# Weight halves by casting and accumulating DMAs, a pair's sums on VectorE, and plain quarters in tiles that stand empty: a two-layer hybrid decoder trunk on one core

## The chip, the cores and the metric

The kernel runs on one NeuronCore of one Trainium2 chip. The metric is device time in microseconds (us) of one execution. Engines are named as the profile names them: PE is TensorE's matmul side and PEld its weight load, DVE is VectorE, ACT is ScalarE, POOL is GpSimd, SP is SyncE. SPq is SP's queue, which issues DMAs here.

## The reference

Two layers over 512 tokens and 1024 channels, all in float32:

```python
h = rmsnorm(x, norm_g[layer])
u = h @ w_in[layer]                 # one projection: q, k, v, z of three mixers and gates ga, gb, gc
ya = forgetting_attention(...)  * silu(za)      # 4 heads, dense causal
yb = dilated_mixture(...)       * silu(zb)      # 6 heads, rotary
yc = banded_attention(...)      * silu(zc)      # 6 query and 2 key heads, rotary, window 128
merged = (sigmoid(ga) * (ya @ w_br_a[layer]) + sigmoid(gb) * (yb @ w_br_b[layer])
          + sigmoid(gc) * (yc @ w_br_c[layer]))
x = x + merged @ w_out[layer]
...
return rmsnorm(x, final_norm_g)
```

## The kernel before, in words

Every product of a weight with activations is made of three float32r matmuls (`mm3`, L127 to L129): a float32 value is split into a rounded half `h` and the rest `lo = x - h`, and `wh*xh + wh*xl + wl*xh` is summed in PSUM. So each weight has to reach SBUF as two tiles, `wh` and `wl`. A weight comes in **chunks** of at most 128x520 (a unit of the input projection is two chunks of 128x512, a branch projection `p` is one of 128x256 or 128x384). The order in which PE uses the chunks is `seq`. One call of `dma()` (L1066) loads chunks ahead through SP into five `raw` tiles, and `split_to()` (L1109) makes the halves up to six chunks ahead of PE: ACT casts `wh <- raw` (L1116) and DVE subtracts `wl <- raw - wh` (L1118; POOL does so for the last output projection). Both rings hold six tiles (`RING`).

In each layer the order of work is: the `v` chunks (eight, with tokens on the PSUM partitions), the `f` chunks (four), then seventeen steps `h` of the attention heads with projections in between, then the merge items. `m_item` ("solo") makes a gate unit `g` (24 matmuls of 512 columns) and a branch product `p` (6 or 9), each in its own PSUM bank of the three called `mm`. Its evacuation is L629 (DVE, `g` times `rbc`), L630 (ACT), L636 or L639 (DVE, with `p`), and for branch 1 a merge into `mg` on POOL (L641).

The last twelve gates of a layer are made two at a time by `pair_steps`, by a Winograd form of Strassen's scheme: seven products of 4 x 3 matmuls of 256 columns instead of eight. A pair uses nine chunks in this order: forms w0, w1, w2, w3, then branch p, then w4, w5, branch p, w6. Forms 0, 1 and 4 are plain quarters of the gate weights (B11, B21, B22); forms 2, 3, 5 and 6 are sums of quarters, made by `source()`: L1101 on DVE, L1103, L1104 and L1106 on POOL. The banks `att` hold the products `a`, `b` and `c`; e1 (L728), e5 (L735) and e2 (L738) are ACT's copies out of them, and product 3 writes the bank that e1 reads. The merge is L707 (POOL, but DVE in the last pair), then ACT's cast L718 and DVE's L719 split the merged gate for the output projection. There are two pairs of branch 1 and four of branch 2 in a layer.

The pairs need sums of activations too. `sums(l, k)`, k = 0 to 3, loads two slices of x (L591), scales them on ACT (L592), forms four sums on POOL and DVE in turn (L600 POOL, L601 DVE, L602 POOL, L603 DVE) and splits them (L607 ACT, L608 DVE). Three of the four stand right before the last two solo items.

Each engine runs its instructions in the order in which they are issued. Python runs ahead, and the tile framework adds the waits and decides from priorities what is issued when (`urgent` raises it).

Of the kernel before, what the change touches and what calls it, by code (L numbers as in the profile page):

```python
# [7 lines left out]
F32 = mybir.dt.float32  # L8
# [19 lines left out]
RING = 6  # L28
RAW = 5
# [35 lines left out]
def tile_trunk(ctx: ExitStack, tc: tile.TileContext, xT, wpk, gT, gfT, bfg, snk,  # L65
# [24 lines left out]
    def tmp():  # L90
        return T([P, S], F32, "tmp", 7)

# [436 lines left out]
    def pv_item(l, h, pair):  # L529
# [30 lines left out]
        def rest():  # L560
            ys = st["ys"]
            nc.vector.tensor_tensor(ys, ys, st["sz", pair], op=ALU.mult)
            if pair < 6:
                yh, yo = T([P, S], F32R, "y", 10), T([P, S], F32R, "y", 10)
# [20 lines left out]
    def sums_x(l, k):  # L585

        src = xT if l == 0 else x1d
        d = []
        for kk in (k, k + 4):
            t = tmp()  # L590
            nc.sync.dma_start(t, src[:, kk, :])  # L591
            nc.scalar.activation(t, t, AF.Copy, scale=g_sb[:, l, kk:kk + 1])  # L592
            d.append(t)
        return d

    def sums(l, k):
        def run():
            a, b = sums_x(l, k)
# [14 lines left out]
    def m_item(l, br, i):  # L613
# [18 lines left out]
        def p2():  # L632
# [7 lines left out]
            if br == 1:  # L640
                nc.gpsimd.tensor_tensor(m, m, gr, op=ALU.add)  # L641
                return
            nc.vector.tensor_tensor(m, m, gr, op=ALU.add)
            pair = []
            for w in range(2):
                n = 2 * i + w
                pair.append(T([P, S], F32R, "qk", 12) if n < 12 else T([P, S], F32R, "y", 10))
            nc.scalar.copy(pair[0], m)
            nc.vector.tensor_tensor(pair[1], m, rd(pair[0]), op=ALU.subtract)
            st["MH", i], st["ML", i] = pair  # L650
        return unit(l, COL["g" + "abc"[br]] + P * i) + [("p", l, br, i)], pe, p1, p2, None

    def pair_steps(l, br, i, last=False):
# [48 lines left out]
        def merge(u, c):  # L702
            def run():
# [3 lines left out]
                (nc.vector if last else nc.gpsimd).tensor_tensor(m, m, gr, op=ALU.add)  # L707
                if br < 2:
                    return
                if ("MH", i + u, l) not in d:  # L710
                    d["MH", i + u, l] = True
                    pair = []
                    for w in range(2):
                        q = 2 * (i + u) + w
                        pair.append(T([P, S], F32R, "qk", 12) if q < 12 else T([P, S], F32R, "y", 10))
# [172 lines left out]
    def layer(l):  # L888
# [79 lines left out]
        for h in range(17):  # L968
            A = items_of(f"a{h}") if h else []
            B = items_of(f"b{h}")  # L970
            if h:
# [4 lines left out]
                if h == 16:  # L976
                    do(sums(l, 3))
# [23 lines left out]
            if h < 15:  # L1001
                do(sscale)
            if h == 16:
                do(vrest)
# [15 lines left out]
        for k in (2, 0, 1):  # L1020
            do(sums(l, k))
        solo(M(1, 2))
        solo(M(1, 3))
# [19 lines left out]

    seq = [c for it in items for c in it[0] or ()]
    loads, at = [], {}
    for i, key in enumerate(seq):
        if key[0] == "w":
            _, l, br, u, form = key
            if form == 0:
                c = [COL["g" + "abc"[br]] + P * (u + w) for w in range(2)]  # L1050
                for name, blk, last in (("B11", ("u", l, c[0], 0), 3), ("B12", ("u", l, c[1], 0), 6),
                                        ("B22", ("u", l, c[1], 1), 6), ("B21", ("u", l, c[0], 1), 8)):
                    loads.append(dict(name=(key[:4], name), blk=blk, tag="raw", last=i + last, since=0))
        else:
            pair = i > 0 and key[0] == "p" and any(k[:3] == ("w", key[1], key[2]) and k[3] in (key[3], key[3] - 1)
                                                   for k in seq)
            since = next(n for n, k in enumerate(seq) if k == ("w", key[1], key[2], key[3] // 2 * 2, 0)) + 1 if pair else 0
            loads.append(dict(name=key, blk=key, tag="sz" if pair else "raw", last=i, since=since))
    order, raw, hl = {"raw": [], "sz": []}, {}, {}
    for n, d in enumerate(loads):  # L1060
        d["turn"] = len(order[d["tag"]])
        order[d["tag"]].append(n)
    ptr = dict(dma=0, split=0)

    def dma(slack=0, most=1 << 30):

        while ptr["dma"] < min(len(loads), most):
            d = loads[ptr["dma"]]
            tag = d["tag"]
            bufs = RAW if tag == "raw" else 2  # L1070
            before = d["turn"] - bufs + (slack if tag == "raw" else 0)
            if ptr["split"] < d["since"]:
                return
            if before >= 0 and loads[order[tag][before]]["last"] >= ptr["split"]:
                return
            o, w = off[d["blk"]]
            t = raw[d["name"]] = T([P, CH], F32, "raw", RAW) if tag == "raw" else T([P, S], F32, "sz", 2)
            nc.sync.dma_start(t[:, :w], bass.AP(tensor=wpk.tensor, offset=wpk.offset + o,
                                                ap=[[w, P], [1, w]]))
            ptr["dma"] += 1  # L1080

    def places(key):

        n = 2 * key[2] + key[3] if key[:2] == ("o", L - 1) else 0
# [167 lines left out]
```

## Time and profile before

| | |
|---|---|
| median of 3 runs (lowest, highest) | 903.9 us (903.22, 904.86) |
| the profiled execution, its own time | 905.74 us |
| its span, first to last instruction | 904.0 us |
| mean granted TensorE clock | 0.988 of full speed |
| DMA traffic | 93.53 MB, mean 103 GB/s |

The profile is of one execution, 1.8 us slower than the median. Shares of busy time are averages over stages; PE is called busy while any of its pipelined matmuls is under way.

### The profile page before, as it was taken

What the parts mean: (1) busy time and instruction counts of PE and PEld (TensorE: products, weight loads), DVE (VectorE), ACT (ScalarE), POOL (GpSimd) and SP (SyncE); (2) the same over time, 40 slices, a digit from 0 to 9 for tenths busy, and PEclk for the clock granted to TensorE, in tenths of its full rate; (3) what the DMA queues carried; (4) which work ended last, traced back from release to release, by engine and by line L of the source; (5) the groups of instructions that cost most, each with busy time, mean ns of one, the idle gap of its engine ahead of it and who ended that gap; (6) DMA issues with size and microseconds to landing.
All of it is one profiled execution on the core that took longest, in us unless ns stands there. A gap on an engine that the chain in (4) does not pass through costs nothing.

```text
span 904.0 us, 14292 instructions
## 1 busy us (share of the span) xinstructions
PE 871.9 (96%) x4866; PEld 754.7 (83%) x4866; DVE 706.2 (78%) x1402; ACT 508.0 (56%) x1072; POOL 212.4 (24%) x162
## 2 busy tenths in 40 slices
PE   9999999999999799899999999999999997998996
PEld 6988888888888599888888888888888876998895
DVE  7668899988787798994446879999878769988643
ACT  7467566655565554554336856576556645544552
POOL 5000231200001545431110012212100035554531
PEclk9999999999999899999999999999999998999998
DMA  6622323323224233345442232233222342322433
GB/s 215 193 84 72 115 70 89 106 78 98 67 63 128 93 117 85 107 130 166 153 129 79 94 92 67 79 104 99 87 88 71 96 137 65 108 85 84 138 95 112
DMA packets 56185, 93.53 MB, mean 103 GB/s; under 512 B 7600, under 2 KB 16176, under 8 KB 56112
## 3 DMA queue, kind: packets, MB, share of 16 engines
q1 hardware_dynamic: 55968, 92.61, 33.4%
q8 instruction: 38, 0.62, 0.3%
q14 instruction: 35, 0.29, 0.1%
q10 hardware_dynamic: 144, 0.01, 0.0%
HBM read 83.15 MB, written 4.19 MB: 97 GB/s over the span
## 4 chain that ended last, share of the span: by engine, by line
PE 78%; issue 7%; DVE 5%; POOL 4%; ACT 3%; DMA 2%; SPq 0%; POOLq 0%; DVEq 0%; ACTq 0%
PE mm L127 18%; PE mm L128 17%; PE mm L129 17%; PE pv L546 4%; PE att L500 3%; PE att L127 3%; PE att L128 3%; PE att L129 3%; PE att L436 2%; PE att L435 2%; DVE wl L1118 2%; ACT wh L1116 1%; PE att L231 1%; PE att L232 1%; PE att L230 1%
## 5 line engine op out<-in xcount | busy, mean ns | idle before, releaser
L1116 ACT CAST wh<-raw 128x512 fp32r<-128x512 f32 (+3 forms) x289 | 172.9, 602 | 191.8 <-PE mm L128 105.4
L1118 DVE TENSOR_TENSOR wl<-raw,wh 128x512 fp32r<-128x512 f32 (+3 forms) x284 | 214.8, 759 | 50.6 <-ACT wh L1116 48.0
L127 PE MATMUL mm<-xh,wh 128*128 128x512 f32 x544 | 217.5, 400 | 0.0
L129 PE MATMUL mm<-xh,wl 128*128 128x512 f32 x544 | 214.8, 395 | 0.0
L128 PE MATMUL mm<-xl,wh 128*128 128x512 f32 x544 | 214.6, 395 | 0.0
L129 PEld LDWEIGHTS mm<-xh,wl 128*128 128x128 f32 x544 | 102.1, 188 | 24.0
L128 PEld LDWEIGHTS mm<-xl,wh 128*128 128x128 f32 x544 | 102.3, 188 | 22.5
L127 PEld LDWEIGHTS mm<-xh,wh 128*128 128x128 f32 x544 | 102.3, 188 | 22.4
L346 POOL TENSOR_TENSOR tmp<-tmp,cos 128x512 f32<-128x512 f32 x20 | 31.4, 1569 | 258.1 <-DVE tmp L338 173.5
L471 ACT ACTIVATE P<-P,ng 128x256 f32<-128x256 f32 (+3 forms) x128 | 66.9, 525 | 31.9 <-DVE ng L469 31.9
L127 PE MATMUL mm<-y,wh 128*128 128x512 f32 (+1 forms) x124 | 49.1, 396 | 12.7 <-DVE tmp L629 12.0
L128 PE MATMUL mm<-y,wh 128*128 128x512 f32 (+1 forms) x124 | 49.0, 395 | 0.3 <-DVE y L719 0.3
L129 PE MATMUL mm<-y,wl 128*128 128x512 f32 (+1 forms) x124 | 48.8, 394 | 0.0
L526 DVE TENSOR_TENSOR PL<-att,PH 128x512 fp32r<-128x512 f32 (+2 forms) x84 | 46.1, 597 | 0.2
L600 POOL TENSOR_TENSOR tmp<-tmp,tmp 128x256 f32<-128x256 f32 x8 | 6.8, 844 | 149.6 <-ACT tmp L592 149.6
L525 ACT CAST PH<-att 128x512 fp32r<-128x512 f32 (+2 forms) x84 | 39.2, 526 | 3.6 <-PE att L500 2.4
L127 PE MATMUL att<-xh,wh 128*128 128x256 f32 x144 | 41.0, 284 | 0.0
L128 PE MATMUL att<-xl,wh 128*128 128x256 f32 x144 | 40.9, 284 | 0.0
L129 PE MATMUL att<-xh,wl 128*128 128x256 f32 x144 | 40.9, 284 | 0.0
L707 POOL TENSOR_TENSOR mg<-mg,tmp 128x512 f32<-128x512 f32 x20 | 32.2, 1610 | 33.1 <-DVE tmp L706 33.1
L489 DVE TENSOR_SCALAR P<-P,den 128x256 f32<-128x256 f32 (+3 forms) x128 | 38.4, 363 | 1.0
L127 PEld LDWEIGHTS mm<-y,wh 128*128 128x128 f32 x124 | 24.1, 194 | 17.6 <-issue 12.8
(257 smaller groups left out, 2094.8 us busy)
## 6 DMA issues: line engine op xcount, KB each, us to landing
raw<-in_wpk_dram SPq DMA_DIRECT2D x232, 256.0 KB, 2.6
tmp<-tmp SPq DMA_DIRECT2D x80, 64.0 KB, 2.0
sz<-in_wpk_dram SPq DMA_DIRECT2D x24, 192.0 KB, 2.4
raw<-in_wpk_dram SPq DMA_DIRECT2D x8, 260.0 KB, 2.6
mg<-in_xT_dram SPq DMA_DIRECT2D x8, 256.0 KB, 5.7
raw<-in_wpk_dram SPq DMA_DIRECT2D x16, 128.0 KB, 2.0
tmp<-in_xT_dram SPq DMA_DIRECT2D x8, 256.0 KB, 3.6
sz<-in_xT_dram SPq DMA_DIRECT2D x8, 256.0 KB, 3.0
```

The lines of the kernel that those rows point to most:

```text
L127: nc.tensor.matmul(ps, wh, xh, start=first, stop=False, skip_group_check=part)
L128: nc.tensor.matmul(ps, wh, xl, start=False, stop=False, skip_group_check=part)
L129: nc.tensor.matmul(ps, wl, xh, start=False, stop=last, skip_group_check=part)
L346: nc.gpsimd.tensor_tensor(t, x, st["cos"], op=ALU.mult)
L471: nc.scalar.activation(pb, pb, AF.Exp, bias=ng[:, i:i + 1], scale=-1.0, accum_out=den[:, i:i + 1])
L489: nc.vector.tensor_scalar(blks[i], blks[i], den[:, i:i + 1], None, op0=ALU.mult)
L525: nc.scalar.copy(hh, bk[:, :n])
L526: nc.vector.tensor_tensor(st["PL"][:, o:o + n], bk[:, :n], rd(hh), op=ALU.subtract)
L546: nc.tensor.matmul(ps[:, q:q + n], v[j], src[:, o:o + n], start=w == 0 and m == 0, stop=w == 1 and m == 3)
L707: (nc.vector if last else nc.gpsimd).tensor_tensor(m, m, gr, op=ALU.add)
L1116: (nc.vector.tensor_copy if i == 0 else nc.scalar.copy)(h[:, :w], r[:, :w])
L1118: eng.tensor_tensor(lo[:, :w], r[:, :w], rd(h[:, :w]), op=ALU.subtract)
```

## The change

The halves of most weight chunks no longer come from one raw tile. A DMA issued by POOL reads the float32 weights and writes them as float32r, which gives `wh`; ACT writes `wl = -wh`; and a second DMA of POOL adds the same weights from DRAM onto `wl`. These are 248 chunks, so 496 DMAs, on POOL's queue. Chunks that stay as before (raw tile by SP, cast by ACT, subtraction) are the `v` and `f` chunks of layer 0, the last output projection's and the forms 2, 3, 5 and 6. Their raw tiles are now tiles that stand empty at that time (`y`, `qk`, `xh`, `xl`) instead of `raw` and `sz`. The ring of `wh` has ten tiles (`RINGH`), that of `wl` seven.

All differences of quarters go to DVE (L1119 after), and so do all four sums of `sums` (L603 to L606 after); the loads of x are issued earlier, and the four `sums` stand farther apart. The merge of branch 2 goes from POOL to DVE (L700 after). Of the last output projection's subtractions half go from POOL to DVE (L1135 after).

```diff
-RING = 6
-RAW = 5
+RING = 7
+RINGH = 10
...
-    def sums_x(l, k):
...
+    def sums_load(l, *ks):
+        def run():
+            src = xT if l == 0 else x1d
+            for k in ks:
+                for kk in (k, k + 4):
+                    t = st["xa", kk] = tmp()
+                    nc.sync.dma_start(t, src[:, kk, :])
+        return run
...
-            nc.gpsimd.tensor_tensor(u[:, T0], a[:, T1], b[:, T1], op=ALU.add)
+            nc.vector.tensor_tensor(u[:, T0], a[:, T1], b[:, T1], op=ALU.add)
             nc.vector.tensor_tensor(u[:, T1], u[:, T0], a[:, T0], op=ALU.subtract)
-            nc.gpsimd.tensor_tensor(v[:, T0], a[:, T0], a[:, T1], op=ALU.subtract)
+            nc.vector.tensor_tensor(v[:, T0], a[:, T0], a[:, T1], op=ALU.subtract)
...
-                (nc.vector if last else nc.gpsimd).tensor_tensor(m, m, gr, op=ALU.add)
+                (nc.vector if br == 2 else nc.gpsimd).tensor_tensor(m, m, gr, op=ALU.add)
...
-                if h == 16:
-                    do(sums(l, 3))
...
+            if h == 15:
+                do(sums_load(l, 3))
             if h == 16:
-                do(vrest)
+                do(sums(l, 3), sums_load(l, 2), vrest, sums(l, 2), sums_load(l, 0))
...
-        for k in (2, 0, 1):
-            do(sums(l, k))
+        do(sums(l, 0), sums_load(l, 1))
         solo(M(1, 2))
+        do(sums(l, 1))
         solo(M(1, 3))
...
+    def load(n):
+
+        while ptr["load"] < min(n, len(seq)):
+            i = ptr["load"]
+            key = seq[i]
+            if is_plain(key) or key[0] == "w" and key[4] == 0:
+                tags, since = raw_slots(key)
+                if not free(tags, since):
+                    return
...
+                    nc.sync.dma_start(t[:, :w], ap)
+            hl[i] = places(key)
+            if not is_plain(key) and not (key[0] == "w" and key[4] in (2, 3, 5, 6)):
+                k = key if key[0] != "w" else quarters(key)[{0: "B11", 1: "B21", 4: "B22"}[key[4]]]
+                ap, w = block(k)
+                nc.gpsimd.dma_start(hl[i][0][:, :w], ap)
+            ptr["load"] += 1
...
-        if form == 3:
-            nc.gpsimd.tensor_tensor(b11, b22, b11, op=ALU.subtract)
-            nc.gpsimd.tensor_tensor(b21, b21, b11, op=ALU.subtract)
-        if form == 5:
-            nc.gpsimd.tensor_tensor(b12, b22, b12, op=ALU.subtract)
-        return (b11, b21, b11, b11, b22, b12, b21)[form]
+        a, b, o = {2: (b12, b11, b11), 3: (b22, b11, b11), 5: (b22, b12, b12), 6: (b21, b11, b21)}[key[4]]
+        nc.vector.tensor_tensor(o, a, b, op=ALU.subtract)
+        return o
...
+                eng = nc.gpsimd if key[:2] == LAST_O and key[3] == 0 else nc.vector
+                eng.tensor_tensor(lo[:, :w], r[:, :w], rd(h[:, :w]), op=ALU.subtract)
+            else:
+                k = key if key[0] != "w" else quarters(key)[{0: "B11", 1: "B21", 4: "B22"}[key[4]]]
+                ap, w = block(k)
+                nc.scalar.activation(lo[:, :w], rd(h[:, :w]), AF.Copy, scale=-1.0)
+                nc.gpsimd.dma_start(lo[:, :w], ap, accum_op=ALU.add)
             ptr["split"] += 1
...
-        split_to(pos + RING)
-        dma(1)
-        pos += len(chunks)
+        load(pos + RINGH if n > 4 else pos + 8)
+        split_to(pos + RING)
+        pos = end
```

What this does to the order of instructions is shown at three places of layer 0.

**DVE at the last solo items.** In before, these twelve rows stand in DVE's queue ahead of and up to the evacuation of solo item (1,2)'s gate, which is the last row (L629, `mm_3256`). L601, L603 and L608 belong to `sums`, L1101 and L1118 to the first pair's weights.

```order
L1118 TENSOR_TENSOR wl_3348<-raw_3147,wh_3347 128x512
L608 TENSOR_TENSOR PL_131<-tmp_3210,PH_130 128x512
L608 TENSOR_TENSOR PL_131<-tmp_3211,PH_130 128x512
L1101 TENSOR_TENSOR raw_3147<-raw_3162,raw_3147 128x512
L1118 TENSOR_TENSOR wl_3352<-raw_3305,wh_3351 128x512
L601 TENSOR_TENSOR tmp_3226<-tmp_3226,tmp_3220 128x256
L603 TENSOR_TENSOR tmp_3227<-tmp_3223,tmp_3226 128x256
L1118 TENSOR_TENSOR wl_3357<-raw_3147,wh_3356 128x512
L608 TENSOR_TENSOR vb_721_3233<-tmp_3226,vb_720_3232 128x512
L608 TENSOR_TENSOR vb_721_3233<-tmp_3227,vb_720_3232 128x512
L1118 TENSOR_TENSOR wl_3387<-raw_3147,wh_3386 128x512
L629 TENSOR_TENSOR tmp_3307<-mm_3256,rbc_560 128x512
```

In the changed kernel the same evacuation is L632 with `mm_3174`, the last row here; L603 to L606 and L611 are one call of `sums`, L632 with `mm_3116` and L642 are the solo item before.

```order
L632 TENSOR_TENSOR tmp_3151<-mm_3116,rbc_557 128x512
L611 TENSOR_TENSOR PL_134<-tmp_3102,PH_133 128x512
L611 TENSOR_TENSOR PL_134<-tmp_3103,PH_133 128x512
L642 SCALAR_TENSOR_TENSOR tmp_3151<-tmp_3151,mm_3141 128x512
L603 TENSOR_TENSOR tmp_3158<-tmp_3112,tmp_3114 128x256
L605 TENSOR_TENSOR tmp_3159<-tmp_3112 128x256
L604 TENSOR_TENSOR tmp_3158<-tmp_3158,tmp_3112 128x256
L606 TENSOR_TENSOR tmp_3159<-tmp_3114,tmp_3158 128x256
L611 TENSOR_TENSOR vb_648_3165<-tmp_3158,vb_647_3164 128x512
L611 TENSOR_TENSOR vb_648_3165<-tmp_3159,vb_647_3164 128x512
L632 TENSOR_TENSOR tmp_3222<-mm_3174,rbc_557 128x512
```

Between two evacuations there is one call of `sums` and no subtraction of a weight that waits for POOL.

**POOL in a pair of branch 1.** Before, one pair is five rows on POOL: three differences of quarters and two merges.

```order
L1106 TENSOR_TENSOR raw_3403<-raw_3423,raw_3403 128x512
L1103 TENSOR_TENSOR raw_3369<-raw_3423,raw_3369 128x512
L1104 TENSOR_TENSOR raw_3427<-raw_3427,raw_3369 128x512
L707 TENSOR_TENSOR mg_2657<-mg_2657,tmp_3401 128x512
L707 TENSOR_TENSOR mg_2500<-mg_2500,tmp_3400 128x512
```

After, it is twelve: L1110 loads a `wh`, L1140 accumulates onto a `wl`, L700 merges. 128x384 marks a branch chunk p.

```order
L1110 DMA wh_3404<-in_wpk_dram 128x384
L1110 DMA wh_3421<-in_wpk_dram 128x512
L1140 DMA wl_3390<-in_wpk_dram 128x512
L1140 DMA wl_3406<-in_wpk_dram 128x512
L1110 DMA wh_3458<-in_wpk_dram 128x384
L1110 DMA wh_3506<-in_wpk_dram 128x512
L1140 DMA wl_3460<-in_wpk_dram 128x384
L700 TENSOR_TENSOR mg_2594<-mg_2594,tmp_3336 128x512
L1140 DMA wl_3478<-in_wpk_dram 128x512
L1110 DMA wh_3530<-in_wpk_dram 128x512
L700 TENSOR_TENSOR mg_2442<-mg_2442,tmp_3335 128x512
L1140 DMA wl_3532<-in_wpk_dram 128x384
```

The accumulations stand behind loads that wait until PE has left a `wh` tile.

**ACT between two pairs of branch 2.** Before, e1 of the next pair (L728) stands behind the cast of a merged gate (L718), which waits for POOL's merge.

```order
L699 ACTIVATE tmp_3759<-tmp_3759 128x512
L1116 CAST wh_3913<-sz_3834 128x384
L718 CAST qk_3895<-mg_1824 128x512
L1116 CAST wh_3938<-raw_3779 128x512
L699 ACTIVATE tmp_3758<-tmp_3758 128x512
L1116 CAST wh_3961<-raw_3717 128x512
L728 COPY tmp_3942<-att_3925 128x256
```

After, at the same place, e1 is L721, the casts of merged gates are L711, and L1139 are the negations, each of which waits for a loaded `wh`.

```order
L692 ACTIVATE tmp_3694<-tmp_3694 128x512
L1133 CAST wh_3798<-y_741_3679 128x512
L1139 ACTIVATE wl_3840<-wh_3779 128x512
L711 CAST qk_3823<-mg_1785 128x512
L692 ACTIVATE tmp_3693<-tmp_3693 128x512
L1133 CAST wh_3839<-y_743_3683 128x512
L721 COPY tmp_3878<-att_3851 128x256
L1139 ACTIVATE wl_3898<-wh_3816 128x384
```

The cast ahead of e1 now waits for a merge on DVE, and among the weights' rows some wait for a DMA of POOL where they waited for a subtraction on POOL.

## Rows read from the trace of the kernel before

**Rows 1.** The page: span, and busy time of each engine.

```profile
span 904.0 us, 14292 instructions
PE 871.9 (96%) x4866; PEld 754.7 (83%) x4866; DVE 706.2 (78%) x1402; ACT 508.0 (56%) x1072; POOL 212.4 (24%) x162
```

**Rows 2.** PE's waits: who waited for whom, us in total, times, longest.

```profile
PE mm L127 <- DVE tmp L629: 12.0, 2, 6.0
PE att L127 <- ACT tmp L728: 7.0, 6, 1.5
PE mm L129 <- POOL vb L1118: 0.8, 1, 0.8
PE mm L127 <- ACT y L718: 0.7, 1, 0.7
PE mm L128 <- DVE y L719: 0.3, 1, 0.3
```

**Rows 3.** PE in order of time around 310 us: start, duration, instruction.

```profile
304.05 0.39 PE L128 MATMUL mm<-xl,wh 128*128 128x512 f32 x1
304.28 0.40 PE L129 MATMUL mm<-xh,wl 128*128 128x512 f32 x1
310.63 0.77 PE L127 MATMUL mm<-y,wh 128*128 128x512 f32 x1 [5.95 <-DVE tmp L629]
...
314.61 0.41 PE L127 MATMUL att<-xh,wh 128*128 128x256 f32 x1
...
316.05 0.28 PE L128 MATMUL att<-xl,wh 128*128 128x256 f32 x1
316.17 0.28 PE L129 MATMUL att<-xh,wl 128*128 128x256 f32 x1
```

**Rows 4.** DVE in order of time, same place.

```profile
303.87 0.94 DVE L601 TENSOR_TENSOR tmp<-tmp,tmp 128x256 f32<-128x256 f32 x1 [1.88 <-POOL tmp L600]
308.35 1.53 DVE L1118 TENSOR_TENSOR wl<-raw,wh 128x512 fp32r<-128x512 f32 x1
309.81 0.68 DVE L629 TENSOR_TENSOR tmp<-mm,rbc 128x512 f32<-128x512 f32 x1
```

**Rows 5.** Busy by stretch: from:to, us, engines' busy time (instructions), granted clock, DMA share, GB/s.

```profile
314.00:316.00 2.00, 2.00 (x9) 1.81 (x9) 2.00 (x4) 1.06 (x2) 0.31 (x1) 0.51 0.00 0
316.00:318.00 2.00, 2.00 (x19) 2.00 (x19) 1.75 (x3) 1.18 (x3) 0.80 (x1) 1.00 0.48 144
362.60:378.50 15.90, 14.35 (x102) 13.35 (x102) 14.17 (x22) 7.80 (x17) 7.67 (x5) 1.00 0.29 91
50.00:280.00 230.00, 229.58 (x1160) 193.18 (x1160) 196.28 (x452) 145.83 (x332) 27.97 (x18) 1.00 0.29 87
404.30:470.90 66.60, 66.60 (x291) 54.10 (x290) 31.07 (x48) 26.25 (x43) 9.90 (x10) 1.00 0.50 155
```

**Rows 6.** ACT in order of time between two pairs of branch 2.

```profile
376.02 0.62 ACT L718 CAST qk<-mg 128x512 fp32r<-128x512 f32 x1 [2.89 <-POOL mg L707]
378.11 0.36 ACT L728 COPY tmp<-att 128x256 f32<-128x256 f32 x1
```

**Rows 7.** Groups by line and shape: busy us, mean ns of one, idle before.

```profile
L1118 DVE TENSOR_TENSOR wl<-raw,wh 128x512 fp32r<-128x512 f32 x252 | 198.2, 789 | 44.7 <-ACT wh L1116 42.3
L707 POOL TENSOR_TENSOR mg<-mg,tmp 128x512 f32<-128x512 f32 x20 | 32.2, 1610 | 33.1 <-DVE tmp L706 33.1
L360 POOL MEMSET qk<- 64x512 f32 x8 | 4.2, 520 | 1.9 <-PE mm L128 1.4 <-DVE wl L1118 0.2
L489 DVE TENSOR_SCALAR P<-P,den 128x256 f32<-128x256 f32 x56 | 17.4, 347 | 0.0
L489 DVE TENSOR_SCALAR P<-P,den 128x512 f32<-128x512 f32 x20 | 9.6, 481 | 0.0
```

**Rows 8.** SP's queue in order of time: one DMA issue with its duration.

```profile
288.85 0.33 SPq L1078 DMA_DIRECT2D sz<-in_wpk_dram  x1
```

**Rows 9.** DMA issues by kind: count, KB each, median us from issue to landing.

```profile
raw<-in_wpk_dram SPq DMA_DIRECT2D x232, 256.0 KB, 2.6
```

More of the change, by code (lines that the diff above doesn't have):

```diff
@@ L91, in tmp, with y_slot @@
         return T([P, S], F32, "tmp", 7)
+    def y_slot(n, dt=F32R):
+        return T([P, CH], dt, f"y{n}")[:, :S]
     def rd(ap):
@@ L563, in rest @@
             if pair < 6:
-                yh, yo = T([P, S], F32R, "y", 10), T([P, S], F32R, "y", 10)
+                yh, yo = (y_slot((2 * pair + w) % 10) for w in range(2))
             else:
@@ L639, in p2 @@
             nc.vector.scalar_tensor_tensor(gr, gr, 1.0, d["p"], op0=ALU.add, op1=ALU.mult)
[L640 to L650, printed above, removed]
+            nc.gpsimd.tensor_tensor(m, m, gr, op=ALU.add)
         return unit(l, COL["g" + "abc"[br]] + P * i) + [("p", l, br, i)], pe, p1, p2, None
@@ L714, in run @@
                         q = 2 * (i + u) + w
-                        pair.append(T([P, S], F32R, "qk", 12) if q < 12 else T([P, S], F32R, "y", 10))
+                        pair.append(qk_tile() if q < 12 else y_slot(q - 8))
                     st["MH", i + u], st["ML", i + u] = pair
@@ L1044, in tile_trunk @@
     seq = [c for it in items for c in it[0] or ()]
-    loads, at = [], {}
-    for i, key in enumerate(seq):
-        if key[0] == "w":
[L1048 to L1080, printed above, removed]
+    where = {key: i for i, key in enumerate(seq)}
@@ new lines, in tile_trunk, with is_plain, block, quarters @@
+    raw, hl, busy = {}, {}, {}
+    ptr = dict(load=0, split=0, used=0)
+    LAST_O = ("o", L - 1)
+    PAIRS = [k[2:4] for k in seq if k[0] == "w" and k[1] == 0 and k[4] == 0]
+    def is_plain(key):
+        return key[:2] in (("v", 0), ("f", 0), LAST_O)
+    def block(key):
+        o, w = off[key]
+        return bass.AP(tensor=wpk.tensor, offset=wpk.offset + o, ap=[[w, P], [1, w]]), w
+    def quarters(key):
+        _, l, br, u, _ = key
+        c = [COL["g" + "abc"[br]] + P * (u + w) for w in range(2)]
+        return dict(B11=("u", l, c[0], 0), B12=("u", l, c[1], 0), B22=("u", l, c[1], 1), B21=("u", l, c[0], 1))
@@ new lines, in raw_slots @@
+    def raw_slots(key):
+        if key[0] == "w":
+            n = PAIRS.index(key[2:4])
+            if key[2:4] <= (2, 0):
+                return ["qk"] * 4, ("p", key[1], 1, 0)
+            return ([f"y{m}" for m in ((2, 3, 8, 9) if key[3] != 4 else (4, 5, 6, 7))],
+                    ("p", key[1], 1, 7))
+        if key[0] == "v":
+            return [f"y{key[2]}"], None
+        if key[0] == "f":
+            return [f"y{(8 + key[2]) % 10}"], None
+        n = (2 * key[2] + key[3]) % 8
+        return [f"xh{n}" if n < 4 else f"xl{n - 4}"], ("w", key[1], 2, 6, 0)
@@ L1082, in places, with free @@
+    def free(tags, since):
+        if since is not None and where[since] >= ptr["used"]:
+            return False
+        return all(t == "qk" or busy.get(t, -1) < ptr["split"] for t in tags)
     def places(key):
-        n = 2 * key[2] + key[3] if key[:2] == ("o", L - 1) else 0
+        n = 2 * key[2] + key[3] if key[:2] == LAST_O else 0
+        h = T([P, CH], F32R, "wh", RINGH) if n < 10 else None
         if n < RING:
-            return T([P, CH], F32R, "wh", RING), T([P, CH], F32R, "wl", RING)
+            return h, None
@@ L1130, in tile_trunk @@
         nc.sync.dma_start(xs[k], xT[:, k, :])
-        dma(0, min(k + 1, RAW))
+        load(min(k + 1, 5))
     split_x(xs[0], 0, 0, 2)
@@ L1157, in tile_trunk @@
             continue
-        split_to(pos + len(chunks))
-        dma()
-        fn([hl.pop(i) for i in range(pos, pos + len(chunks))])
+        end = pos + len(chunks)
+        load(end)
+        split_to(end)
+        assert ptr["split"] >= end, seq[pos]
+        fn([hl.pop(i) for i in range(pos, end)])
+        ptr["used"] = end
         if n < KT - 1:
```

47 lines of the change are left out of this document (22 added, 25 removed).

## The prediction

> **What bounds the kernel now.** First the page: PE is busy for 871.9 of the span's 904.0 us, DVE for 706.2, POOL for 212.4 [rows 1]. So the kernel is bound by PE, and a change that issues the same matmuls can win only where PE waits or runs at the lower clock. The order of PE's rows is the same in both kernels (4,609 rows each). The reader should therefore look at PE's list of waits next. It is short: two waits of 6 us for L629 on DVE, six waits of up to 1.5 us for the copy L728 on ACT (7.0 us together), and three short ones in the tail, 0.8, 0.7 and 0.3 us [rows 2].
>
> The two long ones are at the same place of the two layers. PE stops at 304.7 us and starts again at 310.63 us, in solo item (1,3), because the three `mm` banks are full: the gate of (1,2) has not been read [rows 3]. DVE, which should read it by L629, is busy with what stands ahead of that in its queue: `sums` that wait for POOL, and a `wl` subtraction whose cast waited for a difference made on POOL; L629 itself starts at 309.81 us [rows 4]. After the wait PE runs at the lower clock: the granted clock is 0.51 (1.2 GHz) in 314 to 316 us and 1.00 (2.4 GHz) right after [rows 5]. From 310.63 to 314.61 us stand nine matmuls of 512 columns, 0.442 us apart, against 0.23 at full clock (304.05 to 304.28), and from 314.61 to 316.05 seven of 256 columns, 0.206 us apart against 0.12 [rows 3]. That is 9 x 0.21 + 7 x 0.086 = 2.5 us more. One gap so costs 6.0 + 2.5 = 8.5 us, and the two cost 17.
>
> The wait for L728 comes between pairs of branch 2. The cast L718 waits 2.89 us for a merge on POOL, L728 starts 1.5 us after that cast ends [rows 6], and PE's product 3 needs the bank that L728 reads.
>
> All that the change can give back is then 17 + 7.0 + 1.8 = 25.8 us.
>
> **What it removes.** DVE loses 308 - 68 = 240 `wl` subtractions, 0.79 us each [rows 7], some 190 us, and gains 36 differences, 16 sums and the merges of branch 2, some 40 us. DVE is not the bound, so this alone is worth nothing. What counts is that the L629 of (1,2) no longer has POOL's work ahead of it: in the new order one call of `sums` with no step on POOL stands between two evacuations, so I take the 17 us as won. The merge ahead of e1 goes from POOL (1.61 us [rows 7]) to DVE and its cast no longer holds up e1, so I take the 7.0 us. The tail's waits hang on POOL's `lo` subtractions and merged halves of the last output projection, half of which leave POOL; I take the 1.8 us. ACT's count does not change: each of the 248 negations takes the place of a cast.
>
> **What it adds.** 496 DMAs on POOL, a kind that the trace of before does not have. Two prices are unknown.
>
> *What one DMA costs POOL (c).* An issue on SP's queue takes 0.33 us [rows 8], the dearest POOL row of this size 1.61 us, and the cheapest large POOL row, a MEMSET that reads nothing, 0.52 us [rows 7]. The bounds are 0.33 and 1.6. A DMA's issue reads no tile either, but is more work than one on SP: I take 1.0, the middle. The Trainium skill, "DMA: Bandwidth & Descriptors", section "Latency and other measured facts", gives about 1 us for GpSimd's path to the first byte, for its descriptors are written by software; by that figure the sum would be the same.
>
> *When an accumulation has landed (a).* A plain 256 KB load lands 2.6 us after its issue [rows 9]. An accumulation must read its destination as well, so at most twice that, 5.2 us; I take 3.0 from the end of its issue.
>
> Where does c decide? In a pair of PE work of 14.35 us (84 matmuls of 256 columns and 18 of 512, 102 in all [rows 5]) POOL issues ten DMAs, and in branch 1 also two merges of 1.6 us: 10 + 3.2 = 13.2 us, or 10 us in branch 2. It just fits. Latency is tighter. Take t = 0 where PE ends w6 of a branch 1 pair; a form takes it 1.43 us, a branch chunk 2.1. POOL is then released by PE for the load of the w0 after next (0 to 1), accumulates for the first p (1 to 2, landed at 5; PE uses it at 5.7), merges (to 3.6), accumulates for w4 (to 4.6, landed 7.6; used 7.8), loads (5.6), merges (7.2), accumulates for the second p (8.2, landed 11.2; used 10.7). One margin is negative by 0.5 us, so the four pairs of branch 1 cost 2 us; those of branch 2, with no merges, nothing. Solo items: six DMAs and a merge, 7.6 us, against 33 matmuls x 0.233 = 7.7 us. The output projection of layer 0 with layer 1's `v`: 48 DMAs and six adds of about 1.5, 57 us, in 66.6 us of PE [rows 5]. In the heads' steps of a layer (50 to 280 us, POOL now busy for 28 us [rows 5]) the new order has 138 DMAs, so 166 us in 230. For small misfits in these stages I add 2 us. New waits: 4 us.
>
> The attention steps hold one more doubt. A L489 on DVE takes 347 ns for 256 columns and 481 for 512, so 0.52 ns for each further column, where L1118 takes 1.5 a column [rows 7]; all shapes of it together are 128, 44 us, 22 in a layer. The Trainium skill, "SBUF — State Buffer", section "Who interferes with whom", says that GpSimd cannot write descriptors while DVE is in a 2-port mode, which such tensor_scalars can enter. If POOL stood still beside each L489, it would need 166 + 22 = 188 us of these 230, so the sum stays; the first rival's chance is the higher for it.
>
> **The sum.** 905.7 (the profiled execution's own time) - 25.8 + 4 = 883.9 us. The profiled execution is 1.8 us above the median of the runs; against 903.9 us that is 882.1 us. I forecast 882.
>
> **Rivals.** *POOL's queue becomes the bound* (ends slower). At c = 1.6: pairs of branch 1 take 16 + 3.2 = 19.2 us, 4.85 too many, four times; of branch 2 16 us, 1.65 too many, eight times; ten solo items 11.2 against 7.7 us, less some 16 us that the two rings hold ready; the output projection 86 against 66.6 us. That is 19 + 13 + 19 + 19 = 70 us, and 878 + 70 = 948 us. It decides from about c = 1.4, where the same terms are 11 + 0 + 7 + 10 = 28 us and eat the whole gain. For it speaks that POOL's rows have been slow wherever DVE worked beside them (1.61 us in L707); against it that the issue reads nothing.
>
> *Accumulations land late.* With a = 5.2 us each accumulation of the timetable lands 2.2 us later, and PE waits about 2 us in each of twelve pairs, 24 us; and the DMA engines, at a share of 0.50 for 155 GB/s in the output projection [rows 5], get 6.3 MB more there, or 12.6 if an accumulation counts twice: a share of 0.80 to 1.1, some 7 us over. 878 + 31 = 909 us, slower. It decides from a of about 4.8.
>
> *The long gap stays.* The evacuation of (1,2) now waits for a buffer that POOL's merge of (1,1) has to free, and that merge stands behind three loads and three accumulations, the last load released only when PE ends (1,2)'s gate. If this waits as long as the old one did, only 8.8 us are won: 903.9 - 8.8 + 2 = 897 us. Against it: from that release POOL needs two DMAs and a merge, 3.6 us, and PE needs the bank 7.7 us after it (9 matmuls of p and 24 of a gate).
>
> **Chances.** Forecast 0.56, POOL bound 0.17, late landing 0.13, gap stays 0.10, others 0.04. Within 0.2% (1.8 us, about what a measurement can tell from no change) of 903.9 lies part of the first two rivals: 0.06. Faster is 0.56 + 0.10 = 0.66, slower 0.28. The forecast's own range is 875 to 893 us: 3 us below the sum if there are no new waits, and 11 above if each of ten solo items and twelve pairs waits half a us. The range for 8 in 10 runs from 872 to 918, to take in the late landing and the lower part of POOL's.
>
> **What would show it.** Right: no wait for L632 near 305 and 745 us of the old time, the clock at 1.00 there, no wait for e1 (L721), POOL's issues of about 1.0 us and POOL busy for some 610 us in all (212 now, 94 moved away, 496 added). Wrong: waits of PE for `wl` tiles that a DMA releases, above all in pairs and solo items; POOL without idle time there; ACT's negations waiting for `wh` with e1 behind them; a DMA share near 1 in the output projection.

## The result: faster by 1.8%, and not by the DMA halves

The changed kernel took 888.4 us in the median of four executions, the kernel before 904.15; the ratio is 0.982, with a 95% interval of 0.980 to 0.984, so the gain is small but clear of the noise. One of the four executions took 4,901.7 us, with PE far slower throughout (a matmul of 512 columns shows 1,723 ns for 400) and no cause found; it is left out of the ratio (the other three took 887.5, 887.8 and 889.0 us), and the profile below is of another execution of the same kernel, 888.7 us, from the first experiment.

The page of the changed kernel: span and busy times, the DMA engines' share in 40 slices, and the two large queues (packets, MB, share of the sixteen engines' span).

```profile
span 886.9 us, 14416 instructions
PE 867.9 (98%) x4866; PEld 751.8 (85%) x4866; DVE 568.6 (64%) x1226; ACT 510.3 (58%) x1072; POOL 463.2 (52%) x586
DMA  8697767978989799999997886788798888999413
q0 software_dynamic: 71424, 121.70, 69.0%
q1 hardware_dynamic: 25440, 41.20, 14.1%
```

Against [rows 1], DVE lost 138 us and POOL gained 251. PE's idle time (span less busy) fell from 32.1 to 19.0 us, and its busy time by 4.0, because fewer of its matmuls ran at the lower clock (mean granted clock 0.988 before, 0.992 now). That is the 17.1 us by which the span is shorter. (The last matmul comes 19.0 us earlier; what stands behind it takes 2.0 us more, and the experiment with narrow accumulations shows why.) The `DMA` row is the new thing: the engines that move data are busy in most of the span.

PE's waits, to be held against [rows 2]:

```profile
PE att L130 <- ACT tmp L721: 3.2, 2, 2.8
PE att L130 <- DVE tmp L737: 1.6, 2, 1.4
PE mm L130 <- ACT y L711: 1.2, 2, 0.7
PE mm L131 <- DVE y L712: 0.3, 1, 0.3
```

L632, the old L629, is gone from the list, and with it both waits of 6 us. The copy e1 (L721, the old L728) has two waits instead of six, but one of them is 2.8 us long. The wait for L737, the sum that frees e2's bank, is new. No row of the whole list names a `wl` that a DMA releases.

The windows (from:to, us, busy of each engine, granted clock, DMA share, GB/s): heads' steps, last solo items, two stretches of pairs, output projection, and layer 1's first pair right after the wait of 2.8 us.

```profile
50.00:280.00 230.00, 230.00 (x1163) 193.80 (x1162) 163.19 (x393) 145.40 (x330) 122.68 (x154) 1.00 0.84 177
304.00:318.00 14.00, 13.58 (x94) 12.46 (x93) 11.68 (x19) 7.78 (x16) 11.06 (x14) 1.00 0.74 146
320.00:350.00 30.00, 28.63 (x208) 26.71 (x207) 18.10 (x31) 13.43 (x28) 19.23 (x24) 1.00 0.98 215
350.00:400.00 50.00, 49.50 (x337) 45.10 (x336) 34.91 (x63) 29.21 (x57) 28.74 (x41) 1.00 0.99 215
400.00:460.00 60.00, 60.00 (x260) 48.63 (x259) 11.46 (x16) 23.29 (x37) 39.20 (x51) 1.00 1.09 258
743.50:747.00 3.50, 3.44 (x14) 3.30 (x15) 2.45 (x4) 1.95 (x6) 3.50 (x5) 0.53 1.00 180
```

Where PE once ran at 0.51 of its clock [rows 5] it is now granted 1.00 and stands still for 0.42 us. In the pairs the DMA share is 0.98 and 0.99, where a pair of before had 0.29 [rows 5], and there PE loses 1.4 and 0.5 us. The longest wait has a price of its own behind it: after 2.8 us without work PE is granted 0.53 of its clock in 743.5 to 747 us.

The groups of POOL's two kinds of DMA (busy, mean ns of one, idle before), and then the DMA issues with the median us from issue to landing:

```profile
L1140 POOL DMA_DIRECT2D wl<-in_wpk_dram x248 | 226.4, 934 | 151.7 <-ACT wl L1139 136.7
L1110 POOL DMA_DIRECT2D wh<-in_wpk_dram x248 | 169.6, 697 | 172.1 <-PE mm L132 127.6
...
wh<-in_wpk_dram POOLq DMA_DIRECT2D x196, 256.0 KB, 4.7
wl<-in_wpk_dram POOLq DMA_DIRECT2D x196, 256.0 KB, 5.1
y<-in_wpk_dram SPq DMA_DIRECT2D x32, 256.0 KB, 6.0
```

A cast costs POOL 0.70 us and an accumulation 0.93. SP's plain loads of 256 KB (`y`) now land after 6.0 us; the same load took 2.6 [rows 9].

The wait of 2.8 us, layer 1's first pair, in order of time (engines put together):

```profile
743.56 0.49 PE L130 MATMUL att<-vb,wh 128*128 128x256 f32 x1 [2.81 <-ACT tmp L721]
...
734.39 0.72 ACT L601 ACTIVATE tmp<-tmp,g 128x512 f32<-128x512 f32 x1 [0.74 <-DMA tmp<-x1d]
739.56 0.62 ACT L1133 CAST wh<-qk 128x512 fp32r<-128x512 f32 x1 [1.74 <-DVE qk L1119]
741.97 0.63 ACT L633 ACTIVATE tmp<-tmp 128x512 f32<-128x512 f32 x1 [0.32 <-DVE tmp L632]
743.13 0.37 ACT L721 COPY tmp<-att 128x256 f32<-128x256 f32 x1
...
737.09 1.78 DVE L611 TENSOR_TENSOR vb<-tmp,vb 128x512 fp32r<-128x512 f32 x1
738.79 0.68 DVE L1119 TENSOR_TENSOR qk<-qk,qk 128x512 f32<-128x512 f32 x1
...
736.93 1.39 POOL L643 TENSOR_TENSOR mg<-mg,tmp 128x512 f32<-128x512 f32 x1 [2.74 <-DVE tmp L642]
```

Read it from the top down. PE waits for e1, which stands in ACT's queue behind L633 and casts L1133. A cast waits for a difference of quarters, L1119, and that stands in DVE's queue behind the last call of `sums`, which began late because its load of `x1d` landed late. One subtraction of that call took 1.78 us instead of 0.68, while POOL's merge L643 was running. So the chain begins at a load on SP's queue, not at a DMA of POOL's. The late load shows only 0.74 us of idle time on ACT and the slow subtraction adds 1.1 us, but the lateness is older than this stretch: the sixteen loads of x took 6.5 us to land in the median (3.8 without accumulations, an experiment below), and a later load waits for a tile that an earlier call of `sums` or a merge frees, so the delays add up. The wait for L737 at 348.6 us has the same start: DVE stood idle for 1.63 us, until 343.29, for a `y` load of SP's, and then worked with hardly a stop up to L737 at 348.15.

### The profile page after: what moved, and what is told of

The parts are those of the page before. It is cut to its first block, busy times and chain, and to the rows that moved or that the text cites. A ratio compares the mean times of both kernels' runs of the same rounds, so it can differ in the third digit from the quotient of the medians.

```text
span 4899.9 us, 14416 instructions
## 1 busy us (share of the span) xinstructions
PE 4888.4 (100%) x4866; PEld 3811.2 (78%) x4866; DVE 580.9 (12%) x1226; ACT 528.2 (11%) x1072; POOL 456.1 (9%) x586
## 4 chain that ended last, share of the span: by engine, by line
PE 100%; DVE 0%; ACT 0%; issue 0%; DVEq 0%; ACTq 0%
PE mm L130 22%; PE mm L131 22%; PE mm L132 22%; PE att L131 5%; PE att L130 5%; PE att L132 5%; PE pv L549 4%; PE att L503 4%; PE att L438 2%; PE att L439 2%; PE att L234 2%; PE att L235 2%; PE att L233 2%; PE mm L260 1%; PE mm L262 1%; PE mm L261 1%
## 5 line engine op out<-in xcount | busy, mean ns | idle before, releaser
L130 PE MATMUL mm<-xh,wh 128*128 128x512 f32 x544 | 937.5, 1723 | 0.0
L131 PE MATMUL mm<-xl,wh 128*128 128x512 f32 x544 | 922.0, 1695 | 0.0
L132 PE MATMUL mm<-xh,wl 128*128 128x512 f32 x544 | 920.2, 1692 | 0.0
L132 PEld LDWEIGHTS mm<-xh,wl 128*128 128x128 f32 x544 | 495.8, 911 | 221.0 <-issue 220.6
L130 PEld LDWEIGHTS mm<-xh,wh 128*128 128x128 f32 x544 | 496.8, 913 | 211.4 <-issue 211.4
L131 PEld LDWEIGHTS mm<-xl,wh 128*128 128x128 f32 x544 | 497.6, 915 | 203.5 <-issue 203.5
L1110 POOL DMA_DIRECT2D wh<-in_wpk_dram x248 | 138.1, 557 | 3415.4 <-PE mm L131 2512.4
L1139 ACT ACTIVATE wl<-wh 128x512 fp32r<-128x512 f32 (+3 forms) x248 | 149.6, 603 | 2617.7 <-PE mm L132 2307.2
L1140 POOL DMA_DIRECT2D wl<-in_wpk_dram x248 | 213.7, 881 | 531.3 <-ACT wl L1139 459.6
L130 PE MATMUL mm<-y,wh 128*128 128x512 f32 (+1 forms) x132 | 210.4, 1594 | 0.0
L131 PE MATMUL mm<-y,wh 128*128 128x512 f32 (+1 forms) x132 | 210.4, 1594 | 0.0
L438 PE MATMUL att<-qk,qk 128*128 128x256 f32 (+2 forms) x128 | 153.7, 1201 | 0.0
L131 PEld LDWEIGHTS mm<-y,wh 128*128 128x128 f32 x132 | 122.3, 927 | 35.8 <-issue 35.8
L439 PE MATMUL att<-qk,qk 128*128 128x256 f32 (+2 forms) x128 | 149.9, 1171 | 0.0
L130 PEld LDWEIGHTS mm<-y,wh 128*128 128x128 f32 x132 | 121.3, 919 | 36.0 <-issue 36.0
```

What stands on the lines that cost most here:

```text
L130: nc.tensor.matmul(ps, wh, xh, start=first, stop=False, skip_group_check=part)
L131: nc.tensor.matmul(ps, wh, xl, start=False, stop=False, skip_group_check=part)
L132: nc.tensor.matmul(ps, wl, xh, start=False, stop=last, skip_group_check=part)
L438: nc.tensor.matmul(ps, q[:, qs], kh[:, a:a + n], start=True, stop=False)
L439: nc.tensor.matmul(ps, q2[:, qs], k2[:, a:a + n], start=False, stop=True)
L1110: nc.gpsimd.dma_start(hl[i][0][:, :w], ap)
```

## The experiments

My theory after the first of these profiles: the gain comes from what moved from POOL to DVE, and the DMA halves cost time, since they fill the DMA engines and make every load late. The rivals: the halves bring part of the gain, or they cost it by POOL's queue, or by the accumulations' own landing.

### The parts one by one

**The changed kernel again**, unedited.

> The changed kernel itself once more, for a profile at its usual speed. All theories: 888 us, ratio 0.982. My theory (the three old waits are gone, and the 6 us short of my sum are new waits on POOL's DMAs in pairs and solo items): no wait for L632 near 300 and 735 us, POOL DMA issues of 0.5 to 1.0 us each, and 5 to 10 us of PE waits for wh or wl tiles that a DMA or a negation releases. Rival one (a part of the old gap stays): a PE wait of 2 us or more for L632 and the lower clock behind it. Rival two (late landing): accumulations land 4 us or more after their issue and PE waits in most pairs.

Measured: 891.06 us (888.27 to 892.89), ratio 0.986 [0.984, 0.988]. The gain is 1.2 to 2% in both measurements. The waits for `wh` and `wl` that I expected here, 5 to 10 us of them, are not in the list; the theory above took their place.

**The sums alone**, in the kernel before:

```diff
-            nc.gpsimd.tensor_tensor(u[:, T0], a[:, T1], b[:, T1], op=ALU.add)
+            nc.vector.tensor_tensor(u[:, T0], a[:, T1], b[:, T1], op=ALU.add)
...
-        for k in (2, 0, 1):
-            do(sums(l, k))
+        do(sums(l, 0), sums_load(l, 1))
         solo(M(1, 2))
+        do(sums(l, 1))
```

> The kernel before with one part of the change alone: the four sums on VectorE, their loads earlier and the four calls farther apart. If the long gap is made by POOL's steps in the sums and their place, it closes and the time falls by up to 17 us, to 887 to 890. If the gap is made by VectorE's load (weight subtractions and differences of POOL in its queue), about half of it or more stays: 895 to 904.

Measured: 892.46 us (892.10 to 892.67), ratio 0.987 [0.986, 0.989], between the two outcomes that I had named. The waits for L629 are gone; those for e1 grew from 7.0 to 10.5 us (PE's waits):

```profile
PE att L127 <- ACT tmp L728: 10.5, 8, 1.6
```

**Differences and merges alone**, in the kernel before:

```diff
-                (nc.vector if last else nc.gpsimd).tensor_tensor(m, m, gr, op=ALU.add)
+                (nc.vector if br == 2 else nc.gpsimd).tensor_tensor(m, m, gr, op=ALU.add)
...
-            nc.gpsimd.tensor_tensor(b11, b22, b11, op=ALU.subtract)
-            nc.gpsimd.tensor_tensor(b21, b21, b11, op=ALU.subtract)
+            nc.vector.tensor_tensor(b11, b22, b11, op=ALU.subtract)
+            nc.vector.tensor_tensor(b21, b21, b11, op=ALU.subtract)
...
-            nc.gpsimd.tensor_tensor(b12, b22, b12, op=ALU.subtract)
+            nc.vector.tensor_tensor(b12, b22, b12, op=ALU.subtract)
```

> The kernel before with the differences of quarters and the branch 2 merges on VectorE, and the sums as before. My sum: it wins the 7.0 us of waits behind the merges and leaves the long gap, 896 to 898. If VectorE's queue makes the long gap, the added rows lengthen it: 899 to 906. If a part of the long gap hung on POOL's differences, it shortens: 888 to 894.

Measured: 890.12 us (888.25 to 891.64), ratio 0.985 [0.983, 0.987]. The waits for e1 are gone, the long ones are shorter (12.0 us before):

```profile
PE mm L127 <- DVE tmp L629: 8.7, 2, 5.1
```

**Both, and no DMA halves**: the last two diffs together, weights as before by raw tile, cast and subtraction.

> The kernel before with all parts of the change but the DMA halves, the tiles and the tail: sums, differences of quarters and branch 2 merges on VectorE, weight halves by cast and subtraction. If the DMA halves only cost (new waits), this is faster than the changed kernel: 878 to 886. If VectorE needs the relief of 240 subtractions to carry the sums and differences, it is slower than the changed kernel: 890 to 910.

Measured: 879.06 us (878.61 to 879.72), ratio 0.973 [0.971, 0.974]. This is faster than the changed kernel. The two parts alone gave 1.3 and 1.5%, together 2.7%: they add up. Its page (with the one large DMA queue), and the longest of PE's waits that stand in neither the first 15 nor the last 10 us:

```profile
span 877.9 us, 14215 instructions
PE 865.6 (99%) x4866; PEld 750.8 (86%) x4866; DVE 701.5 (80%) x1466; ACT 510.3 (58%) x1072; POOL 134.3 (15%) x98
...
q1 hardware_dynamic: 55968, 92.61, 34.9%
...
PE mm L129 <- POOL vb L1118: 0.7, 1, 0.7
```

DVE is as busy as before (80%) and PE hardly waits. DVE's load was never the trouble; what stood ahead of what in its queue was.

**The changed kernel with the old sums**: the DMA halves, differences and merges stay, and `sums` goes back to POOL and DVE in turn at its old places (the diff of the sums, reversed).

> The changed kernel with the sums as before (two of four steps on POOL, three calls in a row ahead of the last two solo items). If the sums' part is what closed the long gap, it comes back: 17 us or more on 888, so 903 to 912, the more since POOL's steps of the sums now stand behind DMAs. If the DMA halves alone freed VectorE enough, little comes back: 888 to 893.

Measured: 897.63 us (894.5 to 899.74), ratio 0.993 [0.991, 0.994], again between the two outcomes. The long waits are back though no weight subtraction waits for POOL there, and one row, the only one of its kind in these runs, names an accumulation:

```profile
PE mm L130 <- DVE tmp L632: 9.4, 2, 5.4
...
PE att L132 <- DMA wl<-in_wpk_dram: 0.3, 1, 0.3
```

Beside the differences and merges alone (890.12), the DMA halves cost 7.5 us here; beside the kernel without them (879.06) they cost 9 to 12 us. They give nothing in either. (The tail's edit, below, is in these differences too; the tail of the changed kernel shows 1.0 us of waits, that of the kernel without DMA halves 0.7, so it makes little of them.)

### What of the DMA halves costs the time

**No accumulation**: the changed kernel without its 248 second DMAs.

```diff
                 nc.scalar.activation(lo[:, :w], rd(h[:, :w]), AF.Copy, scale=-1.0)
-                nc.gpsimd.dma_start(lo[:, :w], ap, accum_op=ALU.add)
```

> The changed kernel without its 248 accumulating DMAs (the weights' low halves are then only the negated high halves, a part of the computation left out); loads, negations and all else stay. Profile after: DMA engines at a share of 0.85 to 1.1 in most stages, loads landing 5 to 6 us after issue, no PE wait that a low half ends. If the accumulations' traffic and issues are what costs 10 us against the kernel without DMA halves (it lengthens every other load), the time falls to 879 to 883. If the cast loads of the high halves cost it, it stays at 887 to 891.

Measured: 877.25 us (877.18 to 877.37), ratio 0.971 [0.969, 0.972]. Its page, the windows of the pairs as above, and the `y` loads:

```profile
PE 863.9 (99%) x4866; PEld 750.1 (86%) x4866; DVE 562.6 (64%) x1226; ACT 511.5 (58%) x1072; POOL 249.8 (29%) x338
q0 software_dynamic: 35712, 60.85, 26.8%
...
320.00:350.00 30.00, 30.00 (x222) 28.43 (x221) 21.10 (x36) 16.34 (x33) 10.29 (x15) 1.00 0.53 154
350.00:400.00 50.00, 50.00 (x331) 45.72 (x331) 32.08 (x58) 27.85 (x54) 11.11 (x21) 1.00 0.47 124
...
y<-in_wpk_dram SPq DMA_DIRECT2D x32, 256.0 KB, 4.1
```

Without the accumulations the share in the pairs is halved, PE does not stop there, and SP's loads land after 4.1 us instead of 6.0. The span is 875.2 us, 11.7 less than the changed kernel's: 7.7 us less idle time of PE, 4.0 us less busy time. (The weights' low halves are incomplete in this kernel and in the three like it below, so it is a measuring device and no version to use.)

**Narrow accumulations**: as many DMAs, each behind its negation on the same queue, but 64 columns wide.

```diff
-                nc.gpsimd.dma_start(lo[:, :w], ap, accum_op=ALU.add)
+                o, wd = off[k]
+                ap = bass.AP(tensor=wpk.tensor, offset=wpk.offset + o, ap=[[wd, P], [1, 64]])
+                nc.gpsimd.dma_start(lo[:, :64], ap, accum_op=ALU.add)
```

> The changed kernel with each accumulating DMA cut to 64 of its 256 to 520 columns (the rest of each low half keeps the negated high half, a part of the computation left out). POOL still issues all 496 DMAs in the same order, with as many rows each; the bytes fall by some 50 MB. If POOL's queue (its issues of 0.7 and 0.9 us, in order) costs the 10 us, the time stays at 887 to 891. If the DMA engines' load costs it, the time falls to 879 to 883.

Measured: 879.49 us (878.85 to 880.26), ratio 0.973 [0.972, 0.975]; span 877.9. POOL was busy for 467.7 us, as in the changed kernel. So of the 11.7 us between the two spans 2.7 are there whatever the accumulations' size, and the 9.0 left hang on their bytes.

Of the 2.7 us, 2.25 lie behind the last matmul, where the span still runs for 8.45 us in this kernel and in the changed one, and for 6.20 without accumulations. POOL's last instruction there is a DRAIN. The rows give its line, count, and shortest, median and longest time in ns; the third number is the drain meant. In order: no DMA halves, no accumulations, the changed kernel, narrow accumulations.

```profile
L1247 POOLq DRAIN  x3: 40/82/1517, 872.0 to 877.7; - x3
L1270 POOLq DRAIN  x3: 40/102/4474, 869.5 to 874.9; - x3
L1271 POOLq DRAIN  x3: 40/102/7166, 879.0 to 886.7; - x3
L1273 POOLq DRAIN  x3: 40/93/7171, 870.0 to 877.7; - x3
```

It takes 1.5 us where POOL issued no DMA, 4.5 after 248 and 7.2 after 496, though the last of the 496 had landed 56 us before the drain began. At 248 it ends 0.2 us before the last store of the output lands (874.2 us) and so costs nothing; at 496 it ends 2.4 us after that (886.2 against 883.7). So only 0.5 us are left for POOL's issues and their order in all the work before.

The 9.0 us lie where the DMA engines are full. Set side by side matmul by matmul, the changed kernel falls back by 3.5 us against this one in layer 0's last solo items and pairs and by 5.5 in layer 1's, 4.6 of these at the wait of 2.8 us and the lower clock behind it.

By the bytes there are still two ways: a product waits for its own late `wl`, or the loads of others are late. The idle time of two lines settles part of it. In the changed kernel L601 (ACT, scaling of x's slices) and L1119 (DVE, differences of quarters), both fed by SP's loads, stood idle for:

```profile
  DMA tmp<-x1d: 8.8, 4
  DMA tmp<-in_xT_dram: 6.4, 4
...
  DMA y<-in_wpk_dram: 14.8, 10
  DMA qk<-in_wpk_dram: 6.4, 3
```

Without accumulations L1119's two rows are

```profile
  DMA y<-in_wpk_dram: 3.4, 3
  DMA qk<-in_wpk_dram: 0.2, 1
```

and in the kernel without DMA halves the scaling (L598 there) has 1.3 and 2.5 us. The chain at 743.56 us and these rows show the loads of others late, and the changed kernel's list of PE's waits has none for an accumulation.

**The load without the landing**: in place of each accumulation a copy of the same block to a part of DRAM that nobody reads, and then the same copied twice.

```diff
-                nc.gpsimd.dma_start(lo[:, :w], ap, accum_op=ALU.add)
+                nc.gpsimd.dma_start(spare[i % 24][:, 0, :w], ap)
```

> The changed kernel, but each of the 248 accumulating DMAs is a plain copy of the same weights from DRAM to a part of DRAM that nobody reads, on the same queue of POOL. Left out: the rest of each weight's split (wl is only -wh). So POOL issues as many DMAs and the DMA engines move the bytes, but no product waits for them. If the time lost against the kernel without subtractions by DMA comes from the DMA engines' load, which makes SP's loads land late, the time follows the DMA share: with some 0.7 in the stage of 320 to 400 us (0.5 without the second DMAs, 0.98 with accumulations) I expect 877 to 882 us and y loads that land in 4.1 to 5 us. If it comes from the accumulations' own landing, for which products wait, it stays at 877 to 878 us whatever the share.

> The same with each block copied twice by one DMA, so twice the bytes (the same part of the computation is left out). Theory of the shared DMA engines: share near 1 in 320 to 400 us, y loads landing in 5 to 6 us, 884 to 892 us, and PE waits for e1 (L721) or for the e2 sum (L737) in the pairs again, though no product waits for a second DMA. Theory of the accumulations' own landing: 877 to 880 us and no such waits.

Measured: 886.24 us (885.79 to 886.34), ratio 0.980 [0.978, 0.981], and 904.03 us (902.09 to 906.17), ratio 1.000 [0.998, 1.001]. Both came out above what I expected, and for a reason that I had not seen: a copy waits for no engine's work, so POOL issued the copies far ahead of the weights that they stood for. With single copies the share was near 1 for the first 290 us and 0.50 in 320 to 350 us, so the pairs were not tested, and PE had no wait there. Against the kernel without accumulations it had lost 7.1 us by 297 us and lost nothing more before the last matmul; the drain behind it adds the other 2.3. With doubled copies the load reached through layer 0 and ended before layer 1's pairs. PE's waits and windows of that kernel, pairs of layer 0 and then of layer 1:

```profile
PE att L131 <- DVE tmp L738: 7.1, 3, 3.5
PE mm L131 <- DVE tmp L633: 1.7, 1, 1.7
...
300.00:400.00 100.00, 91.21 (x595) 82.62 (x594) 65.93 (x118) 52.97 (x102) 58.04 (x80) 0.98 0.99 333
...
755.00:775.00 20.00, 20.00 (x149) 18.95 (x148) 10.60 (x19) 9.46 (x20) 8.88 (x13) 1.00 0.38 96
775.00:845.00 70.00, 69.01 (x494) 64.37 (x493) 51.56 (x85) 37.48 (x74) 15.24 (x22) 1.00 0.48 140
```

At a share of 0.99 PE lost 8.8 of 100 us in layer 0's solo items and pairs; at 0.38 to 0.48, in layer 1, 1.0 of 90, which is the tail's wait for the last merge. No product waited for a copy, so such waits need no accumulation's landing. The 1.7 us for L633 are of the changed kernel's kind: ACT stood idle for 3.77 us for a load of x by SP, DVE for 4.26 us for ACT, and L633 stood behind the sums in DVE's queue. It is not a clean measure of their size: here the `wh` loads, which stand behind the copies in POOL's queue, were late too (ACT's L1140 stood idle for 5.3 us for one of them just before the wait of 3.5 us), and these copies moved more bytes than the accumulations.

### A version that should have been faster

The kernel without DMA halves, with half of the last output projection's subtractions given to DVE, as the change has it:

```diff
-            eng = nc.gpsimd if key[:2] == ("o", L - 1) else nc.vector
+            eng = nc.gpsimd if key[:2] == ("o", L - 1) and key[3] == 0 else nc.vector
```

> The kernel without DMA halves (sums, differences and merges on VectorE) and with half of the last output projection's subtractions on VectorE, as in the changed kernel. Its one PE wait that POOL ends in the tail is 0.66 us. If that wait is worth its length the time is 878.3, within 0.1% of 879.1 and the fastest of all; if VectorE's rows there delay the first products, 879 to 881.

Measured: 883.27 us (882.66 to 883.69), ratio 0.977 [0.976, 0.979]: 4.2 us slower than without the edit. PE's waits in the tail:

```profile
PE mm L129 <- POOL vb L1118: 1.3, 2, 0.7
PE mm L129 <- POOL xl L1118: 1.3, 2, 0.6
PE mm L129 <- POOL va L1118: 0.6, 1, 0.6
```

This is above both outcomes that I had named. Five waits of some 0.6 us, where there was one of 0.7. PE waits for POOL's half, though POOL has less to do: 134.3 us of work became 123.0. I take it that the subtractions on DVE now stand behind evacuations that wait for PE, and so hold the five `raw` tiles longer, from which the next casts come; no run tells this apart. The best complete kernel of this study is the one at 879.06 us.

## Why the prediction was right, and where its sizes were off

I forecast 882 us, with 872 to 918 for 8 in 10; 888.4 lies inside, and inside the forecast's own range of 875 to 893.

**The gain, 25.8 us: right.** The kernel that has these parts and no DMA halves is 26.1 us shorter in span than the profile of before (904.0 to 877.9), and 24.7 by the medians (903.76 to 879.06). The split was not as I had it. I put 17 us on the long gap and 8.8 on the rest; alone, the sums give 11.5 us (1.27% by the ratio 0.9873), since e1 then waits longer, and the differences and merges 13.6 (1.50%, 0.9850), since they also shorten the long gap. The tail's 1.8 us is only partly won in the changed kernel: 0.8 us of it (POOL's `lo`) is gone, and L711 and L712 still cost 0.7 and 0.3 us there.

**DVE's relief is worth nothing by itself: right.** With it, and no accumulations, the time is 877.25 us; without it 879.06. At most 1.8 us. (DVE lost 224 subtractions, from 284 to 60; the 308 and 68 that I took hold POOL's as well.)

**POOL's price c: taken too high.** 0.70 and 0.93 us, 0.82 in the mean, for the 1.0 taken; POOL is busy for 463 us, not 610. The first rival needed 1.4, and with all 496 issues but narrow accumulations the time is 879.49 us. POOL's queue is not the bound. In the heads' steps POOL is busy for 122.7 of 230 us and PE for all 230.00, so what the Trainium skill says in "SBUF — State Buffer", section "Who interferes with whom", on descriptors beside a 2-port mode cost PE nothing that this trace shows.

**The landing a: mis-sized, 3.0 for about 4.2.** An accumulation lands 5.1 us after its issue, and the issue takes 0.93. That is nearer to my upper bound of 5.2 than to what I took, and short of the 4.8 from which I let it decide. With c and a as measured my timetable gives the three accumulations of a branch 1 pair 0.1, 0.5 and 0.9 us too late, so a wait of some 0.9 us for `wl` in each of four pairs. It was too strict: PE's list has none.

**New costs of 4 us: too small, and of another kind.** They are 25.8 - 17.1 = 8.7 us. 2.0 of them lie behind the last matmul (8.46 us to the end of the span, 6.50 before), where POOL's drain, which my sum does not have, ends the program; the other 6.7, net, are waits and the lower clock. My 4 us stood for late accumulations and small misfits on POOL's queue, and PE's list shows neither; that new waits came at all was right, but not for my reason. The term that is missing is the DMA engines' time in the pairs. I looked at their share in the output projection alone, where my second rival's 0.80 to 1.1 came true (1.09 in 400 to 460 us) and cost PE nothing; in the pairs I counted only POOL's issues. It can be worked out from the queues' rows. Accumulations took 69.0% of 886.9 us less 26.8% of 875.2, 377 us (each a us in which all sixteen engines are busy), for 60.85 MB: 6.2 us per MB. Casts took 235 us for as many, 3.9 per MB, and plain loads 34.9% of 877.9, 306 us, for 92.61 MB: 3.3 per MB. A pair of branch 1 loads four quarters (1.05 MB) and makes three forms and two branch chunks by both DMAs (1.18 MB each): 3.5 + 4.6 + 7.3 = 15.4 us of all engines, against 14.35 us of PE. By this estimate the engines cannot keep up with PE, which fits their share of 0.98 to 0.99 there, and the loads of `sums` and of the quarters fall behind with them. That an accumulation counts about twice I had written down, for another stage.

So the second rival was half right: the DMA engines fill up, but PE does not wait for late accumulations in twelve pairs (24 us). It waits a few times, for e1 and for the sum that frees e2's bank, behind loads of SP that are late for the same reason. The Trainium skill, "DMA: Bandwidth & Descriptors", section "Issuing engines are not separate DMA queues", says that DMAs run on the same sixteen engines whichever engine starts them; the rows agree, since SP's `y` loads land after 6.0 us beside the accumulations and after 4.1 without them.

**The long gap stays: this rival fell.** No wait for L632 in the changed kernel.

What stays open: the size of the cost from one execution to the next. The changed kernel's runs lie between 887 and 893 us, those of the kernel without DMA halves within 1.1 us, and I did not find what sets the difference from one run to the next.

## What to carry to other kernels

When a change has several parts, ask of each what wait it removes before counting what work it saves: here DVE lost 138 us of work for at most 1.8, while the order and the engine of a few rows gave some 25. A DMA that casts or accumulates takes work from a compute engine and gives it to the sixteen DMA engines, so make their balance for each stage (MB by us per MB, against PE's time in that stage), not over the whole span. When that balance goes over, look for the damage at the loads of others.

## What the chip showed beyond that

An accumulating DMA took 1.9 times the DMA engines' time of a plain load per byte (6.2 against 3.3 us per MB), a casting one 1.2 times. With accumulations the engines were full at 215 GB/s (share 0.98), with plain copies on the same queue at 333 (0.99), so GB/s alone does not tell whether they are full.

A DVE subtraction of 128x512 took 1.78 us, for 0.68 elsewhere, while a merge of the same size ran on POOL (736.93 to 738.32 us). It stood in the chain of the longest new wait. The kernel without DMA halves has the like (L1118 at 731.34 us, 1.78 us beside a merge), and there PE did not wait for it.

POOL's DRAIN at the end grows with the DMAs that it issued in the whole program: 1.5, 4.5 and 7.2 us for 0, 248 and 496 of them, and 9.5 where 248 of the 496 copied their block twice.
